# A split weight's low part: one VectorE subtraction, or a ScalarE negative and an adding DMA

## The chip, the cores and the metric

The kernel runs on one core of a Trainium2 chip. Its time is the device time of one execution in microseconds (us); the number given for a kernel is the median of several executions. A profile is one execution recorded by the hardware profiler.

The engines in the profile are PE (TensorE; PEld is its loading of weights into the array), DVE (VectorE), ACT (ScalarE), POOL (GpSimd) and SP (which here only starts transfers). Each works through its own list of instructions in order and waits on semaphores for the others.

## The reference

Two layers of a decoder trunk on 256 positions of width 1024, all in float32. In each layer:

```python
h = h + hybrid_mixer(rmsnorm(h), ...)   # retention and an SSD scan side by side, merged by gates
h = h + swiglu(rmsnorm(h), ...)         # gate and up of width 2816, then down
```

and a last rmsnorm. The mixer multiplies the normed input by one wide matrix `w_in` and cuts the product into `q, k` (1024 columns each), `v, g_ret, z` (2048 each), `xbc` (3072), `dt` (32) and two gates (1024 each). What matters here is `xbc`: it goes through a causal convolution of four taps along the positions and a silu, and is cut into `xs` (2048 columns), `bm` and `cm` (512 each) for the scan:

```python
xbc = jax.nn.silu(causal_dwconv(xbc, conv_w, conv_b))
xs, bm, cm = jnp.split(xbc, [SSD_INNER, SSD_INNER + SSD_BC], axis=-1)
```

## The kernel before

**Float32 by halves.** TensorE multiplies in a format (fp32r) that keeps fewer bits than float32. So every operand is split into a high part, rounded to fp32r, and a low part, the rest. A product is the sum of three: high by high, high by low, low by high. A piece of weights is 128 x 1024 numbers (512 KB). It is loaded from memory into a tile `raw` by a DMA on SP's queue (line 488), then split in `split_piece`: ScalarE copies it into `wh`, which rounds it (line 506), and VectorE writes `wl = raw - wh` (line 527).

**Jobs.** The weights are cut into jobs. The ones of the convolution and of q and k are called `fm` jobs: 256 columns of `w_in`, in two pieces of four blocks of 128 rows each. `fm_job` runs two halves of 128 columns. In each half it goes through the eight row blocks k = 0 to 7, and for each k does a matmul of `wh` with high and low input side by side (512 columns, line 988; line 991 for the last one, which closes the half) and one of `wl` with the high input (256 columns, line 989). The first piece serves k = 0 to 3 and the second k = 4 to 7, in both halves. A half has eight matmuls of line 989; the fifth is the first that needs the `wl` of the second piece.

A layer's mixer list has 20 fm jobs: four `bc`, four `q`, four `k` and eight `xs` (named by group and half: `("xs", 0, 0)` to `("xs", 3, 1)`). From the first `q` on the order is q, k, xs in turn four times, then the `g` jobs with the other four `xs` jobs between them, then `ret`. The list ends with `z`, `ssd` and `wo`, and the FFN's jobs follow.

**Sevens.** Some products are done by a seven-product scheme, whose weight sums are built by `wino_sums`. Some of these sums are made by VectorE; others by a DMA that POOL issues and that adds a piece from memory to a tile already filled (line 416, `accum_op=ALU.add`). These are the only adding transfers before the change, 48 of them, all into float32 tiles.

**Buffers.** There are four `raw` buffers and seven pairs of `wh` and `wl` (`HB = 7`, semaphore `hlS`). Pieces take the pairs in the order of the jobs (`turn.before.taken`), so a piece can be split as soon as the piece seven places ahead of it has been used by TensorE. A `raw` buffer is given back when the split is done.

**Order.** The order of each engine's instructions is planned when the kernel is built, by a small event simulation (`Flow`). Each stream of work yields an `Op` with an engine, a cost in ns and a priority; the free engine takes the ready `Op` of the lowest number. Transfers are costed by `fl.transfer`, on a single queue. The order that comes out is fixed; on the chip only the waits decide when things run. A changed cost or a moved operation may therefore change the order of everything behind it.

**A form that exists but is not used.** `split_piece` takes a `src`. With it, ScalarE writes the negative of `wh` into `wl`, POOL issues a DMA that adds the weights from memory, and the low part is there when the DMA has landed. Jobs whose index is in a tuple `apart` get `src`; before the change each of these tuples is empty.

Of the kernel before, what the change touches and what calls it, by code (L numbers as in the profile page):

```python
# [16 lines left out]
P = 128  # L17
# [175 lines left out]
def trunk_kernel(  # L193
# [4 lines left out]
):  # L198
    nc = tc.nc
    HB, RB, TAIL, WARM = 7, 4, 5, 2  # L200
    APART, LATE = (), 2500.0
    SLOW, MT_SLACK = 1500.0, 800.0
    ADDS = 600.0
    ZS_PR, SAVE, DEC_AT = 1.0, 2000.0, 9000.0
    PR0, SLACK = 1.6, 2500.0
    BESIDE = (8, 10, 12, 14, 11, 11, 9, 24, 44, 46)
    APARTS, SUMS_PR = {}, 3.5
    cp = ctx.enter_context(tc.tile_pool(name="cp", bufs=1))
    wp = ctx.enter_context(tc.tile_pool(name="wp", bufs=HB))
    big = ctx.enter_context(tc.tile_pool(name="big", bufs=4))  # L210
# [80 lines left out]
    ALONE = ("11", "t1", "t2", "22", "t3", "21", "t4")  # L291


    AMID = ("*", "*", "*", "*", "11", "*", "t1", "*", "t2", "22", "*", "t3", "*", "21", "*", "t4")

    SMID = ("*", "*", "11", "*", "t1", "*", "t2", "22", "*", "t3", "21", "t4")


    RMID = ('*', '*', '*', '*', '*', '*', '11', '*', 't1', 't2', '22', 't3', '21', 't4')
    RET_FIRST, RET_APART, RET_PR = (decS, new_dec), (), 0.0  # L300

    class Turn:
        def __init__(self):
# [2 lines left out]
    def group(*adds):  # L306

        of = len(jobs)
        got_turns, got_specs, stars = [], [], []
        for add in adds:  # L310
            t, f, at = add(of)
            if stars:

                t, f = ([(stars[i] if i < len(stars) else 1.0 + i, v) for i, (_, v) in enumerate(e)] for e in (t, f))
            stars = stars or at
            got_turns += t
            got_specs += f
        for into, got in ((turns, got_turns), (specs, got_specs)):
            for _, v in sorted(got, key=lambda e: e[0]):
                if into is turns and turns:  # L320
                    v.before = turns[-1]
                into.append(v)
# [152 lines left out]
    def out_srcs(w):  # L475
        return [(w[k0 : k0 + P, :], 1, D) for k0 in range(0, w.shape[0], P)]
# [14 lines left out]
            raw = yield Op("sp", 450, load, job)  # L491
            fl.spawn(land(raw, fl.transfer(512 * k * n, 4 * k * n)))

    def split_piece(raw, m, turn, pr, src=None):

        if turn.before:
            yield turn.before.taken  # L500
        yield hlS
        fl.set(turn.taken)

        def split_h():
            wh = wp.tile([P, D], F32R, tag="wh", name="wh")
            nc.scalar.activation(out=wh[:, :m], in_=raw[:, :m], func=AF.Copy)  # L506
            return wh

        wh = yield Op("act", 0.833 * m + 92, split_h, pr)

        def negative():
            wl = wp.tile([P, D], F32R, tag="wl", name="wl")
            nc.scalar.activation(out=wl[:, :m], in_=wh[:, :m].bitcast(F32), func=AF.Copy, scale=-1.0)
            return wl

        def add(wl):
            nc.gpsimd.dma_start(out=wl[:, :m], in_=src, accum_op=ALU.add)

        if src is not None:
            wl = yield Op("act", 0.833 * m + 92, negative, pr)  # L520
            yield Op("pool", 1050, lambda: add(wl), pr)
            yield fl.transfer(512 * m, 4 * m, 2.2) - ADDS
            return wh[:, :m], wl[:, :m]

        def split_l():
            wl = wp.tile([P, D], F32R, tag="wl", name="wl")
            nc.vector.tensor_tensor(out=wl[:, :m], in0=raw[:, :m], in1=wh[:, :m].bitcast(F32), op=ALU.subtract)  # L527
            return wl

        wl = yield Op("dve", 1.04 * m + 69, split_l, pr)  # L530
        return wh[:, :m], wl[:, :m]

    def splitter(turn, k, n, ev, job, src, sem):
        def land(raw, landed):
            yield landed
            wh, wl = yield from split_piece(raw, k * n, turn, job - 0.7, src)
            fl.release(sem)
            fl.set(ev, tuple(a.rearrange("p (k n) -> p k n", k=k) for a in (wh, wl)))
        return land

# [516 lines left out]
    def out_wino(op, nk, at, tag, order, post, add, ops):  # L1057
# [74 lines left out]
        for t in range(NT):  # L1132
            for n in range(2):
# [5 lines left out]

    FFN = [[("plain", 0)],
           [("fm", 1)],
           [("seven", (2,), ("t3", "t4"))],
           [("fm", 3)],
           [("seven", (4,), ("t3", "t4"))],
           [("fm", NPAIR)]]
    DIRECT = ()
    DOWN_APART = ()


    MIXER = [("v", 0), ("gr", 0), ("bc", 0, 0), ("v", 1), ("bc", 0, 1), ("v", 2), ("bc", 1, 0), ("v", 3),
# [5 lines left out]

    TM = {"v": 0, "g": 4, "z": 8, "gs": 12}
    FM = {"q": 0, "k": 4, "xs": 8, "bc": 16}  # L1160


    MIXERS = [MIXER[:2] + [MIXER[i ^ 1] for i in range(2, 10)] + MIXER[10:], MIXER]

    def add_layer_jobs(l):
        def srcs_of(kind, *at):
            if kind == "gr":
                return tm_srcs(w_gr[l, at[0]])
            if kind in FM:
                return fm_srcs(w_fm[l, FM[kind] + at[0] + (at[0] + at[1] if len(at) > 1 else 0)])  # L1170
            if kind in ("ret", "ssd", "wo"):
                return out_srcs({"ret": ret_out, "ssd": ssd_out, "wo": w_o}[kind][l])
            return tm_srcs(w_tm[l, TM[kind] + at[0]], kper=1 if l == 0 and (kind, *at) == ("v", 0) else 2)

        def adds_of(kind, *at, order=MIXED):
            if kind == "seven":
                c = TM[at[0]] + at[1]
                return [sevens(w_tm[l, c], w_tm[l, c + 1], added=at[2], order=order, slots=None)]
            return [plain((srcs_of(kind, *at), APARTS.get((kind, *at), ())))]

        for m in MIXERS[l]:
            if m == ("ret",):
                group(sevens(w_rw[l, 0], w_rw[l, 1], added=("t3", "t4"), order=RMID, first=RET_FIRST),
                      plain((out_srcs(ret_out[l])[8:], RET_APART)))
            elif m == ("ssd",):
                group(sevens(w_sw[l, 0], w_sw[l, 1], added=("t3", "t4"), order=SMID, slots=(ccS, new_cc)),
                      plain((out_srcs(ssd_out[l])[8:], ())))
            elif isinstance(m, tuple):
                for add in adds_of(*m, order=ALONE):
                    group(add)  # L1190
            else:
                group(*(chain(*(a for j in stream for a in adds_of(*j))) for stream in m))
        for members in FFN:
            adds = []
            for kind, *at in members:
                if kind == "seven":
                    adds.append(chain(*(sevens(w_gate_up[l, 0, c], w_gate_up[l, 1, c], added=at[1], order=ALONE if len(members) == 1 else ASIDE,
                                               slots=(ccS, new_cc)) for c in at[0])))
                elif kind == "fm":
                    adds.append(plain(*((srcs, APART) for c in at for srcs in gf_srcs(l, c))))  # L1200
                else:
                    adds.append(plain(*((srcs, APART) for c in at for srcs in gate_up_srcs(l, c))))
            group(*adds)
        lone = [s for k, s in enumerate(out_srcs(w_down[l])) if k // 4 not in (DW, DW + 1)]
        group(sevens(w_dw[l, 0], w_dw[l, 1], added=("t3", "t4"), order=AMID, slots=(ccS, new_cc)),
              plain((lone, DOWN_APART)))

    def params(l, done):
        prm = sp.tile([P, 3, NH], F32, tag="prm", name="prm", bufs=1)
# [21 lines left out]
    def layer(l, mix, nxt, opening=None):  # L1231
# [537 lines left out]
            to = yield gated[t]  # L1769
            yield tt(512, j, to[:, nsl], u, sgr[t][:, nsl], ALU.mult)  # L1770

        run["ret"] = lambda: out_wino(yr, 16, 0, "O", RMID, ret_post, add_r, rops)


        yz = Operand(SG, ["Y", "Y", "C", "C"])
# [108 lines left out]
        def ssd_job():  # L1884
            for i in range(2):
                xT.drop(i)
            for t in range(NT):
                fl.spawn(restore(t))
            fl.spawn(ffn.start(at_job[0]))
            fl.spawn(ffn.sums(at_job[0] + 2))  # L1890
            return out_wino(yz, 16, 0, "A", SMID, ssd_post, add_m, zops)

        run["ssd"] = ssd_job

# [113 lines left out]
                return [m for c in at for m in fm_pair(c)]  # L2008
            return [((lambda m=m: tm_job(ffn.xT, m)), 1) for c in at for m in pair(c)]

        last = max(i for i, g in enumerate(FFN) for kind, *_ in g if kind == "seven")
        for i, members in enumerate(FFN):
            if i == 0:
                yield from tm_pair(ffn.xT, *((m, 512, 2) for m in pair(members[0][1])))
            else:
                yield from together(*[ffn_jobs(*m) for m in members])
            if i == last:
                ffn.drop_sums()
# [6 lines left out]

        ops = {q: Event() for q in ALONE}
        fl.spawn(seven_sums(ops, gu, (DW, DW + 1), "D", at_job[0] - 1.2))
        yield from out_wino(gu, FF // P, DW, "D", AMID, add_to(nxt), add_h, ops)

    def rotary_half(rotary, dst, which, done):  # L2030
        part = Event()
# [189 lines left out]
```

## Time and profile before

| | |
|---|---|
| times of three executions | 1252.75, 1253.32, 1255.91 us; median 1253.32 |
| span of the profiled execution | 1251.4 us, from its first to its last instruction (its time as the others are measured is not given beside it) |
| instructions | 17609 |
| granted TensorE clock | 0.999 in the mean |
| DMA | 266.27 MB, in the mean 213 GB/s |

The page gives busy times by engine, groups of instructions by line, and the chain of work that ended last. Other views used below: the timeline (instructions in order, with the idle time before each and what ended it in brackets), the waits (who waited for whom, with total, number and longest), and windows (busy time by engine in given stretches). PE's matmuls overlap in these records: each stands with some 0.39 us, while the next begins 0.23 us after it.

### The profile page before, as it was taken

What the parts mean: (1) busy time and instruction counts of PE and PEld (TensorE: products, weight loads), DVE (VectorE), ACT (ScalarE), POOL (GpSimd) and SP (SyncE); (2) the same over time, 40 slices, a digit from 0 to 9 for tenths busy, and PEclk for the clock granted to TensorE, in tenths of its full rate; (3) what the DMA queues carried; (4) which work ended last, traced back from release to release, by engine and by line L of the source; (5) the groups of instructions that cost most, each with busy time, mean ns of one, the idle gap of its engine ahead of it and who ended that gap; (6) DMA issues with size and microseconds to landing.
All of it is one profiled execution on the core that took longest, in us unless ns stands there. A gap on an engine that the chain in (4) does not pass through costs nothing.

```text
span 1251.4 us, 17609 instructions
## 1 busy us (share of the span) xinstructions
PE 1241.9 (99%) x6286; PEld 1052.4 (84%) x6286; DVE 1108.2 (89%) x1516; ACT 882.7 (71%) x1305; POOL 71.1 (6%) x92
## 2 busy tenths in 40 slices
PE   9999999999999999999999999999999999999997
PEld 8889888888888888888888898888888888888886
DVE  6998989789999979999788888888899998899995
ACT  6866876977776666776586676878877674776753
POOL 0000000001012001001000000000010110010000
PEclk9999999999999999999999999999999999999999
DMA  8758555456768658877776475555577786688872
GB/s 293 248 146 284 184 180 174 153 194 192 253 238 226 229 178 231 297 212 219 249 257 227 124 256 167 188 172 163 208 186 234 243 234 213 225 209 249 289 204 86
DMA packets 76343, 266.27 MB, mean 213 GB/s; under 512 B 8768, under 2 KB 9024, under 8 KB 76256
## 3 DMA queue, kind: packets, MB, share of 16 engines
q1 hardware_dynamic: 68416, 237.25, 55.7%
q0 software_dynamic: 7552, 27.38, 11.8%
q8 instruction: 49, 0.80, 0.2%
q10 hardware_dynamic: 288, 0.52, 0.1%
q14 instruction: 38, 0.31, 0.1%
HBM read 262.96 MB, written 2.16 MB: 212 GB/s over the span
## 4 chain that ended last, share of the span: by engine, by line
PE 92%; ACT 3%; issue 2%; DMA 1%; DVE 0%; POOL 0%; SPq 0%; POOLq 0%; ACTq 0%
PE acc L543 19%; PE acc L544 19%; PE acc L545 19%; PE acc L988 15%; PE acc L989 9%; PE tr L640 2%; PE yps L1700 2%; PE acc L991 2%; ACT wh L506 1%; ACT seg L1668 1%; PE acc L1422 1%; PE tr L1593 1%; PE ips L1687 1%; DMA raw<-in_w_tm_dram 1%; DMA raw<-in_w_gr_dram 0%
## 5 line engine op out<-in xcount | busy, mean ns | idle before, releaser
L506 ACT ACTIVATE wh<-raw 128x1024 fp32r<-128x1024 f32 (+2 forms) x388 | 397.0, 1035 | 150.6 <-PE acc L545 36.3
L527 DVE TENSOR_TENSOR wl<-raw,wh 128x1024 fp32r<-128x1024 f32 (+2 forms) x388 | 458.9, 1196 | 48.5 <-ACT wh L506 46.6
L988 PE MATMUL acc<-xT,wh 128*128 128x512 f32 x840 | 304.2, 400 | 0.0
L989 PE MATMUL acc<-xT,wl 128*128 128x256 f32 x960 | 251.6, 281 | 0.0
L543 PE MATMUL acc<-wh,xT 128*128 128x512 f32 (+1 forms) x568 | 220.6, 388 | 0.0
L545 PE MATMUL acc<-wh,xT 128*128 128x512 f32 (+1 forms) x568 | 216.1, 380 | 0.0
L544 PE MATMUL acc<-wl,xT 128*128 128x512 f32 (+1 forms) x568 | 216.1, 380 | 0.0
L989 PEld LDWEIGHTS acc<-xT,wl 128*128 128x128 f32 x960 | 181.2, 189 | 10.1
L988 PEld LDWEIGHTS acc<-xT,wh 128*128 128x128 f32 x840 | 158.0, 188 | 32.2
L544 PEld LDWEIGHTS acc<-wl,xT 128*128 128x128 f32 x568 | 106.7, 188 | 20.4 <-issue 1.2
L543 PEld LDWEIGHTS acc<-wh,xT 128*128 128x128 f32 x568 | 106.7, 188 | 19.8 <-issue 1.6
L545 PEld LDWEIGHTS acc<-wh,xT 128*128 128x128 f32 x568 | 106.6, 188 | 19.5
L506 ACT ACTIVATE wh<-raws 128x1024 fp32r<-128x1024 f32 x80 | 83.5, 1056 | 31.7 <-DVE raws L230 12.5
L527 DVE TENSOR_TENSOR wl<-raws,wh 128x1024 fp32r<-128x1024 f32 x80 | 96.4, 1222 | 8.9 <-ACT wh L506 8.7
L543 PE MATMUL acc<-wh,A 128*128 128x512 f32 x224 | 89.8, 401 | 0.2
L545 PE MATMUL acc<-wh,A 128*128 128x512 f32 x224 | 87.4, 390 | 0.0
L544 PE MATMUL acc<-wl,A 128*128 128x512 f32 x224 | 87.3, 390 | 0.0
L233 DVE SCALAR_TENSOR_TENSOR cc<-cc,cv 128x255 f32<-128x255 f32 (+1 forms) x144 | 67.3, 479 | 3.0 <-ACT cc L223 2.1
L543 PE MATMUL acc<-wh,C 128*128 128x512 f32 (+1 forms) x152 | 59.2, 389 | 0.0
L544 PE MATMUL acc<-wl,C 128*128 128x512 f32 (+1 forms) x152 | 58.3, 384 | 0.2 <-DVE wl L527 0.2
L545 PE MATMUL acc<-wh,C 128*128 128x512 f32 (+1 forms) x152 | 58.2, 383 | 0.0
L223 ACT ACT_TABLE_LOAD x41 | 52.6, 1283 | 6.1 <-DVE cc L233 5.4
(197 smaller groups left out, 2006.8 us busy)
## 6 DMA issues: line engine op xcount, KB each, us to landing
raw<-in_w_tm_dram SPq DMA_DIRECT2D x104, 512.0 KB, 4.2
raw<-in_w_fm_dram SPq DMA_DIRECT2D x80, 512.0 KB, 4.3
raw<-in_w_gf_dram SPq DMA_DIRECT2D x40, 512.0 KB, 4.5
raw<-in_w_gate_up_dram SPq DMA_DIRECT2D x32, 512.0 KB, 5.8
raw<-in_w_down_dram SPq DMA_DIRECT2D x28, 512.0 KB, 4.5
raw<-in_w_gr_dram SPq DMA_DIRECT2D x24, 352.0 KB, 3.7
seg<-acs SPq DMA_DIRECT2D x16, 512.0 KB, 4.9
raw<-in_ret_out_dram SPq DMA_DIRECT2D x16, 512.0 KB, 4.3
```

Of the source, the lines that this page charges most:

```text
L223: return Op("act", cost, lambda: nc.scalar.activation(out=out, in_=in_, func=func, **kw), pr, TABLES.get(func))
L233: return Op("dve", 1.04 * n + 130, lambda: nc.vector.scalar_tensor_tensor(out=out, in0=in0, scalar=scalar, in1=in1, op0=op0, op1=op1), pr)
L506: nc.scalar.activation(out=wh[:, :m], in_=raw[:, :m], func=AF.Copy)
L527: nc.vector.tensor_tensor(out=wl[:, :m], in0=raw[:, :m], in1=wh[:, :m].bitcast(F32), op=ALU.subtract)
L543: nc.tensor.matmul(ps, lhsT=lh, rhs=rh, start=first, stop=False, **kw)
L544: nc.tensor.matmul(ps, lhsT=lh, rhs=rl, start=False, stop=False, **kw)
L545: nc.tensor.matmul(ps, lhsT=ll, rhs=rh, start=False, stop=last, **kw)
L640: nc.tensor.transpose(out=ps[:, j * P : (j + 1) * P], in_=src[:, j * P : (j + 1) * P], identity=ident)
L988: nc.tensor.matmul(a, lhsT=wh[:, k % 4, fsl], rhs=x[:, k % 4, :, :], start=k == 0, stop=False)
L989: nc.tensor.matmul(a[:, :SEQ], lhsT=wl[:, k % 4, fsl], rhs=xh[:, k % 4, :], start=False, stop=False)
L991: nc.tensor.matmul(a, lhsT=wh[:, k % 4, fsl], rhs=x[:, k % 4, :, :], start=False, stop=True)
L1700: nc.tensor.matmul(ps[:, i * HD : (i + 1) * HD], lhsT=sg[:, i, :], rhs=xdt[:, i * HD : (i + 1) * HD], start=True, stop=True)
```

## The change

The low part of the second piece of all 16 `xs` jobs (eight in each layer) is made with `src`. The rest of the diff turns constants into tables by layer that hold the same values (the mixer lists, the FFN lists, the orders of the sevens). Cut to what acts:

```diff
-    APARTS, SUMS_PR = {}, 3.5
+    APARTS, SUMS_PR = {(0, 'xs', 0, 0): (1,), (0, 'xs', 0, 1): (1,), ..., (1, 'xs', 3, 1): (1,)}, 3.5
...
-    def split_piece(raw, m, turn, pr, src=None):
+    def split_piece(raw, m, turn, pr, src=None, sem=None):
...
         if src is not None:
             wl = yield Op("act", 0.833 * m + 92, negative, pr)
+            if sem:
+                fl.release(sem)
             yield Op("pool", 1050, lambda: add(wl), pr)
             yield fl.transfer(512 * m, 4 * m, 2.2) - ADDS
             return wh[:, :m], wl[:, :m]
...
-            wh, wl = yield from split_piece(raw, k * n, turn, job - 0.7, src)
-            fl.release(sem)
+            wh, wl = yield from split_piece(raw, k * n, turn, job - 0.7, src, sem)
+            if src is None:
+                fl.release(sem)
...
-            return [plain((srcs_of(kind, *at), APARTS.get((kind, *at), ())))]
+            return [plain((srcs_of(kind, *at), APARTS.get((l, kind, *at), ())))]
```

With `src`, a `raw` buffer is now given back after the negative, not after the transfer.

For each of these pieces one instruction of VectorE goes (line 527), and there come one of ScalarE, one DMA issue on POOL's queue, and one transfer of 512 KB that reads the weights a second time and adds them to `wl` in place.

More of the change, by code (lines that the diff above doesn't have):

```diff
@@ L200, in trunk_kernel @@
     HB, RB, TAIL, WARM = 7, 4, 5, 2
-    APART, LATE = (), 2500.0
+    LATE = 2500.0
     SLOW, MT_SLACK = 1500.0, 800.0
@@ L206, in trunk_kernel @@
     BESIDE = (8, 10, 12, 14, 11, 11, 9, 24, 44, 46)
-    APARTS, SUMS_PR = {}, 3.5
+    APARTS, SUMS_PR = {(0, 'xs', 0, 0): (1,), (0, 'xs', 0, 1): (1,), (0, 'xs', 1, 0): (1,), (0, 'xs', 1, 1): (1,), (0, 'xs', 2, 0): (1,), (0, 'xs', 2, 1): (1,), (0, 'xs', 3, 0): (1,), (0, 'xs', 3, 1): (1,), (1, 'xs', 0, 0): (1,), (1, 'xs', 0, 1): (1,), (1, 'xs', 1, 0): (1,), (1, 'xs', 1, 1): (1,), (1, 'xs', 2, 0): (1,), (1, 'xs', 2, 1): (1,), (1, 'xs', 3, 0): (1,), (1, 'xs', 3, 1): (1,)}, 3.5
     cp = ctx.enter_context(tc.tile_pool(name="cp", bufs=1))
@@ L291, in trunk_kernel @@
     ALONE = ("11", "t1", "t2", "22", "t3", "21", "t4")
[L294 to L300, printed above, removed]
+    AMIDS = [('*', '*', '*', '*', '11', '*', 't1', '*', 't2', '22', '*', 't3', '*', '21', '*', 't4'), ('*', '*', '*', '*', '11', '*', 't1', '*', 't2', '22', '*', 't3', '*', '21', '*', 't4')]
+    SMIDS = [('*', '*', '11', '*', 't1', '*', 't2', '22', '*', 't3', '21', 't4'), ('*', '*', '11', '*', 't1', '*', 't2', '22', '*', 't3', '21', 't4')]
+    RMIDS = [('*', '*', '*', '*', '*', '*', '11', '*', 't1', 't2', '22', 't3', '21', 't4'), ('*', '*', '*', '*', '*', '*', '11', '*', 't1', 't2', '22', 't3', '21', 't4')]
+    ADDED = {(0, 'ret'): ('t3', 't4'), (0, 'ssd'): ('t3', 't4'), (0, 'down'): ('t3', 't4'), (1, 'ret'): ('t3', 't4'), (1, 'ssd'): ('t3', 't4'), (1, 'down'): ('t3', 't4')}
+    RET_FIRST, RET_PR = (decS, new_dec), 0.0
     class Turn:
@@ L1138, in out_wino @@
                 fl.spawn(done(t, n))
[L1142 to L1147, printed above, removed]
-    DIRECT = ()
-    DOWN_APART = ()
-    MIXER = [("v", 0), ("gr", 0), ("bc", 0, 0), ("v", 1), ("bc", 0, 1), ("v", 2), ("bc", 1, 0), ("v", 3),
[5 rows of a table removed]
+    FFNS = [[[('plain', 0)], [('fm', 1)], [('seven', (2,), ('t3', 't4'))], [('fm', 3)], [('seven', (4,), ('t3', 't4'))], [('fm', 5)]], [[('plain', 0)], [('fm', 1)], [('seven', (2,), ('t3', 't4'))], [('fm', 3)], [('seven', (4,), ('t3', 't4'))], [('fm', 5)]]]
+    DIRECT = ()
+    MIXER0 = [('v', 0), ('gr', 0), ('v', 1), ('bc', 0, 0), ('v', 2), ('bc', 0, 1), ('v', 3), ('bc', 1, 0), [[('seven', 'gs', 0, ('t3',))], [('gr', 1), ('gr', 2)]], ('bc', 1, 1), ('q', 0), ('k', 0), ('xs', 0, 0), ('q', 1), ('k', 1), ('xs', 0, 1), ('q', 2), ('k', 2), ('xs', 1, 0), ('q', 3), ('k', 3), ('xs', 1, 1), ('g', 0), ('xs', 2, 0), ('g', 1), ('xs', 2, 1), ('g', 2), ('xs', 3, 0), ('xs', 3, 1), ('g', 3), ('ret',), ('z', 0), ('z', 1), ('z', 2), ('z', 3), ('ssd',), ('wo',)]
+    MIXER1 = [('v', 0), ('gr', 0), ('bc', 0, 0), ('v', 1), ('bc', 0, 1), ('v', 2), ('bc', 1, 0), ('v', 3), ('bc', 1, 1), [[('seven', 'gs', 0, ('t3',))], [('gr', 1), ('gr', 2)]], ('q', 0), ('k', 0), ('xs', 0, 0), ('q', 1), ('k', 1), ('xs', 0, 1), ('q', 2), ('k', 2), ('xs', 1, 0), ('q', 3), ('k', 3), ('xs', 1, 1), ('g', 0), ('xs', 2, 0), ('g', 1), ('xs', 2, 1), ('g', 2), ('xs', 3, 0), ('xs', 3, 1), ('g', 3), ('ret',), ('z', 0), ('z', 1), ('z', 2), ('z', 3), ('ssd',), ('wo',)]
+    MIXERS = [MIXER0, MIXER1]
     TM = {"v": 0, "g": 4, "z": 8, "gs": 12}
     FM = {"q": 0, "k": 4, "xs": 8, "bc": 16}
-    MIXERS = [MIXER[:2] + [MIXER[i ^ 1] for i in range(2, 10)] + MIXER[10:], MIXER]
     def add_layer_jobs(l):
@@ L1178, in adds_of @@
                 return [sevens(w_tm[l, c], w_tm[l, c + 1], added=at[2], order=order, slots=None)]
-            return [plain((srcs_of(kind, *at), APARTS.get((kind, *at), ())))]
+            return [plain((srcs_of(kind, *at), APARTS.get((l, kind, *at), ())))]
         for m in MIXERS[l]:
             if m == ("ret",):
-                group(sevens(w_rw[l, 0], w_rw[l, 1], added=("t3", "t4"), order=RMID, first=RET_FIRST),
-                      plain((out_srcs(ret_out[l])[8:], RET_APART)))
+                group(sevens(w_rw[l, 0], w_rw[l, 1], added=ADDED[l, "ret"], order=RMIDS[l], first=RET_FIRST),
+                      plain((out_srcs(ret_out[l])[8:], APARTS.get((l, "ret"), ()))))
             elif m == ("ssd",):
-                group(sevens(w_sw[l, 0], w_sw[l, 1], added=("t3", "t4"), order=SMID, slots=(ccS, new_cc)),
-                      plain((out_srcs(ssd_out[l])[8:], ())))
+                group(sevens(w_sw[l, 0], w_sw[l, 1], added=ADDED[l, "ssd"], order=SMIDS[l], slots=(ccS, new_cc)),
+                      plain((out_srcs(ssd_out[l])[8:], APARTS.get((l, "ssd"), ()))))
             elif isinstance(m, tuple):
@@ L1192, in add_layer_jobs @@
                 group(*(chain(*(a for j in stream for a in adds_of(*j))) for stream in m))
-        for members in FFN:
+        for members in FFNS[l]:
             adds = []
@@ L1199, in add_layer_jobs @@
                 elif kind == "fm":
-                    adds.append(plain(*((srcs, APART) for c in at for srcs in gf_srcs(l, c))))
+                    adds.append(plain(*((srcs, APARTS.get((l, kind, c), ())) for c in at for srcs in gf_srcs(l, c))))
                 else:
-                    adds.append(plain(*((srcs, APART) for c in at for srcs in gate_up_srcs(l, c))))
+                    adds.append(plain(*((srcs, APARTS.get((l, kind, c), ())) for c in at for srcs in gate_up_srcs(l, c))))
             group(*adds)
         lone = [s for k, s in enumerate(out_srcs(w_down[l])) if k // 4 not in (DW, DW + 1)]
-        group(sevens(w_dw[l, 0], w_dw[l, 1], added=("t3", "t4"), order=AMID, slots=(ccS, new_cc)),
-              plain((lone, DOWN_APART)))
+        group(sevens(w_dw[l, 0], w_dw[l, 1], added=ADDED[l, "down"], order=AMIDS[l], slots=(ccS, new_cc)),
+              plain((lone, APARTS.get((l, "down"), ()))))
     def params(l, done):
@@ L1770, in add_r @@
             yield tt(512, j, to[:, nsl], u, sgr[t][:, nsl], ALU.mult)
-        run["ret"] = lambda: out_wino(yr, 16, 0, "O", RMID, ret_post, add_r, rops)
+        run["ret"] = lambda: out_wino(yr, 16, 0, "O", RMIDS[l], ret_post, add_r, rops)
         yz = Operand(SG, ["Y", "Y", "C", "C"])
@@ L1890, in ssd_job @@
             fl.spawn(ffn.sums(at_job[0] + 2))
-            return out_wino(yz, 16, 0, "A", SMID, ssd_post, add_m, zops)
+            return out_wino(yz, 16, 0, "A", SMIDS[l], ssd_post, add_m, zops)
         run["ssd"] = ssd_job
@@ L2009, in ffn_jobs @@
             return [((lambda m=m: tm_job(ffn.xT, m)), 1) for c in at for m in pair(c)]
-        last = max(i for i, g in enumerate(FFN) for kind, *_ in g if kind == "seven")
-        for i, members in enumerate(FFN):
+        last = max(i for i, g in enumerate(FFNS[l]) for kind, *_ in g if kind == "seven")
+        for i, members in enumerate(FFNS[l]):
             if i == 0:
@@ L2027, in layer @@
         fl.spawn(seven_sums(ops, gu, (DW, DW + 1), "D", at_job[0] - 1.2))
-        yield from out_wino(gu, FF // P, DW, "D", AMID, add_to(nxt), add_h, ops)
+        yield from out_wino(gu, FF // P, DW, "D", AMIDS[l], add_to(nxt), add_h, ops)
     def rotary_half(rotary, dst, which, done):
```

5 rows, old and new, of the table MIXER are left out of this document.

## The prediction, made before the changed kernel was run

> **What bounds the kernel now.** I read the page's first two parts, then TensorE's own waits, then the stretches in which the 16 changed jobs are made and used.
>
> ```profile
> span 1251.4 us, 17609 instructions
> PE 1241.9 (99%) x6286; PEld 1052.4 (84%) x6286; DVE 1108.2 (89%) x1516; ACT 882.7 (71%) x1305; POOL 71.1 (6%) x92
> ```
>
> TensorE is busy for 1241.9 of 1251.4 us. The 9.5 us that are left lie almost all at the two ends, as the first and the last TensorE row of the timeline show: nothing runs before 1.32 us, and the last matmul ends at 1244.03 + 0.39 = 1244.42, 7.0 us before the end. That is 8.3 us, so about 1.2 us is open in between.
>
> ```profile
> 1.32 5.91 PE L2094 MATMUL idle<-zeros 128*128 128x384 f32 x19 [1.32 <-DVE mhalf L2071]
> ...
> 1244.03 0.39 PE L545 MATMUL acc<-wh,Y 128*128 128x512 f32 x1
> ```
>
> Busy time hides short waits, because a matmul's end is modelled and overlaps the next. So I also read what TensorE's weight loads wait for. Over the whole run the one wait for a VectorE split (line 527) is 0.8 us in two cases:
>
> ```profile
> PEld acc L544 <- DVE wl L527: 0.8, 2, 0.5
> ```
>
> The changed jobs lie between 112 and 290 us (layer 0) and 729 and 908 us (layer 1). The waits inside these two stretches, and the busy time in six windows that cover them (columns: window, length, then busy time and count of each engine, the last three granted clock, DMA share and GB/s):
>
> ```profile
> PEld acc L543 <- ACT sil L223: 1.0, 2, 0.5
> PEld acc L543 <- issue: 0.5, 2, 0.2
> PEld acc L544 <- issue: 0.5, 2, 0.2
> PEld acc L1422 <- issue: 0.4, 1, 0.4
> ...
> 112.00:175.00 63.00, 62.91 (x360) 55.08 (x359) 53.85 (x88) 46.51 (x75) 1.84 (x2) 1.00 0.64 212
> 175.00:240.00 65.00, 65.00 (x353) 55.69 (x352) 53.15 (x84) 52.23 (x99) 3.56 (x2) 1.00 0.55 170
> 240.00:290.00 50.00, 49.88 (x267) 41.98 (x266) 45.98 (x69) 41.85 (x68) 0.00 (x0) 1.00 0.57 190
> ...
> sum 357.00, PE 356.67 PEld 307.06 DVE 303.66 ACT 280.46 POOL 8.36; mean PE 59.45 PEld 51.18 DVE 50.61 ACT 46.74 POOL 1.39
> ```
>
> TensorE is idle for 0.33 of 357 us there. In layer 0 its weight loads wait 2.4 us in all, and none of it for VectorE; the largest share is for ScalarE (1.0 us). VectorE, the engine that is relieved, is 85% busy in these windows, but TensorE does not wait for it.
>
> **The change, part by part.** Each of the 16 xs jobs has two pieces of weights. For the second one, the difference raw minus wh is no longer a VectorE instruction; ScalarE writes -wh into wl, and a DMA issued by POOL reads the weights from memory again and adds them to wl.
>
> ```profile
> L506 ACT ACTIVATE wh<-raw 128x1024 fp32r<-128x1024 f32 (+2 forms) x388 | 397.0, 1035 | 150.6 <-PE acc L545 36.3 <-DMA raw<-in_w_tm_dram 25.6 <-issue 13.8
> L527 DVE TENSOR_TENSOR wl<-raw,wh 128x1024 fp32r<-128x1024 f32 (+2 forms) x388 | 458.9, 1196 | 48.5 <-ACT wh L506 46.6
> ```
>
> *VectorE, removed.* 16 instructions of 1.2 us: 19 us less, of 303.66 in the windows (85% to 80%). Worth nothing on the path, as TensorE has no wait for VectorE there.
>
> *ScalarE, added.* 16 negatives. None exists before; the nearest row is the split of the same 128x1024 shape (line 506, 1.04 us in the mean, 1.06 in the single rows below). That is 17 us more: 280.46 to 297 of 357, 79% to 83%. The cover is ScalarE's idle time, and the tightest place is the end of the stretch, where TensorE does wait for ScalarE (the 1.0 us above, for sil). The last two negatives of a layer come by the split at 250.04. The idle times from there up to the wait stand in square brackets; the row of a window, the last, shows how full ScalarE (23.88 of 25 us) is behind them, and the row before it, of the chain, is the sil that TensorE waits for:
>
> ```profile
> 250.04 1.06 ACT L506 ACTIVATE wh<-raw 128x1024 fp32r<-128x1024 f32 x1 [1.30 <-PE acc L545]
> 251.44 0.60 ACT L223 ACTIVATE cc<-cc,cv 128x256 f32<-128x256 f32 x1 [0.34 <-DVE cc L230]
> 252.76 1.06 ACT L506 ACTIVATE wh<-raw 128x1024 fp32r<-128x1024 f32 x1 [0.72 <-PE acc L545]
> 255.48 1.06 ACT L506 ACTIVATE wh<-raw 128x1024 fp32r<-128x1024 f32 x1 [1.66 <-PE acc L545]
> ...
> 261.95 0.60 ACT L223 ACTIVATE C<-tr 128x512 f32<-128x512 f32 x1 [1.32 <-PE tr L1593]
> ...
> 264.59 0.60 ACT L223 ACTIVATE A<-tr 128x512 fp32r<-128x512 f32 x1 [1.56 <-PE tr L640]
> 266.24 1.06 ACT L506 ACTIVATE wh<-raw 128x1024 fp32r<-128x1024 f32 x1 [1.04 <-PE acc L988]
> ...
> 286.17 0.50 ACT sil L223
> ...
> 265.00:290.00 25.00, 24.88 (x121) 20.33 (x120) 21.43 (x33) 23.88 (x44) 0.00 (x0) 1.00 0.60 209
> ```
>
> After 251.1 that is 0.34 + 0.72 + 1.66 + 1.32 + 1.56 + 1.04 = 6.6 us, against 2.1 us for both negatives. So ScalarE is back in step by 267 us, ahead of the full stretch that ends in the wait. Cost: nothing; if that cover were gone, 2.1 us in each layer (a rival below).
>
> *POOL, added.* 16 DMA issues. The issues of the same kind before the change (line 416), one whole group, the landing times of all of line 416, and one that directly follows a split:
>
> ```profile
> L416 POOL DMA_DIRECT2D cc<-in_w_gate_up_dram x8: 854/865/913, 483.5 to 1147.8; - x8
> ...
> DMA to landing us min/median/max: 5.1/5.6/9.2
> ...
> 296.38 0.86 POOL L416 DMA_DIRECT2D raw<-in_w_rw_dram  x1 [0.24 <-ACT wh L506]
> POOL rr L243 <- DVE ms L238: 140.7, 4, 77.3
> ```
>
> 14 us of POOL's time, where it works for 8.36 us in 357. What stands behind such an issue on POOL's queue is the four rr instructions of a layer, and they wait 140.7 us for VectorE anyway; a microsecond more reaches nobody.
>
> *Latency of the low part: the step on which the forecast rests.* It was wh, then 1.2 us on VectorE. It becomes wh, 1.06 us on ScalarE, 0.24 us to POOL, and 5.6 us from issue to landing: 6.9 us after wh instead of 1.2 or more. TensorE first needs it in the fifth matmul of line 989 of the job (a job's half ends with a matmul of line 991). I matched pieces by counting the rows of lines 506 and 989 in the order of the job list. The tightest of the 16 is the first xs job of each layer, then the fourth:
>
> ```profile
> 123.14 1.06 ACT L506 ACTIVATE wh<-raw 128x1024 fp32r<-128x1024 f32 x1 [0.70 <-DMA raw<-in_w_fm_dram]
> ...
> 132.25 0.40 PE L991 MATMUL acc<-xT,wh 128*128 128x512 f32 x1
> 134.12 0.28 PE L989 MATMUL acc<-xT,wl 128*128 128x256 f32 x1
> ...
> 742.08 2.25 ACT L506 ACTIVATE wh<-raw 128x1024 fp32r<-128x1024 f32 x2
> 753.60 0.28 PE L989 MATMUL acc<-xT,wl 128*128 128x256 f32 x1
> ...
> 226.47 1.07 ACT L506 ACTIVATE wh<-raw 128x1024 fp32r<-128x1024 f32 x1
> 240.04 0.28 PE L989 MATMUL acc<-xT,wl 128*128 128x256 f32 x1
> ```
>
> Layer 0, first job: wh ends at 124.20, the issue can begin at 125.50, and the weight load of the matmul at 134.12 comes some 0.2 us before it, at 133.9. The landing may take 8.4 us. Layer 1: wh ends at 743.14 (the row holds two; this piece is the first), issue at 744.44, needed at 753.4: 9.0 us. Layer 0, fourth job: wh ends at 227.54, issue at 228.84, needed at 239.8: 11.0 us. The 13 others have at least as much as that. With the median landing the slack is 2.8, 3.4 and 5.4 us. At the longest landing of the trace, 9.2, TensorE would wait 0.8 and 0.2 us: 1.0 in the whole run. Bounds of this step: 0 and 1.0 us; a gain is excluded, since it only makes wl later. I take 0, as 5.6 is the median of the same issues.
>
> *DMA engines, added.* 16 transfers of 512 KB.
>
> ```profile
> q1 hardware_dynamic: 68416, 237.25, 55.7%
> q0 software_dynamic: 7552, 27.38, 11.8%
> 125.00:131.00 6.00, 6.00 (x36) 5.21 (x35) 5.96 (x12) 3.95 (x7) 0.00 (x0) 1.00 0.84 272
> ```
>
> POOL's queue took 11.8% of 1251.4 for 27.38 MB: 5.4 us for a MB, so 2.8 us of all 16 engines for each of the 16 (plain loads on SP's queue take 1.5). That is 45 us in 357: the shares of 0.55 to 0.64 rise to 0.68 to 0.77. Room is left, least of all at the first job, where the share from 125 to 131 us is 0.84 already; there the add and the raw loads behind it slow each other. This is why I keep the longest landing as a bound. The raw loads of the following jobs have a lead like those above and lose at most 2.8 us of it.
>
> *SP's queue.* A raw buffer comes free after wh instead of after VectorE's instruction, so 16 loads may start 1.2 us or more sooner. Worth nothing, since TensorE does not wait for them.
>
> *Order.* The builder plans each engine's order by a cost model, and every choice after the first changed piece can fall otherwise. The tables hold the same jobs in the same order. I take 0, and 1 us to either side, by the 1.2 us that is open inside the run and the 1.0 us of possible lateness.
>
> A rule of the Trainium skill speaks against the change. The page SBUF — State Buffer, section "SBUF: two separate sides", warns that POOL cannot write the descriptors of its DMAs while VectorE runs an instruction that uses both of its ports. By that rule an issue could be held for one VectorE instruction, 1.2 us, and a landing would take 6.8 us, still inside the 8.4. The trace does not show it: with VectorE 89% busy the issues of the group above took 854 to 913 ns, all alike.
>
> *Sum.* 0 on TensorE's path, 1251.4 us of span again. The times shown for the runs are 1252.75, 1253.32 and 1255.91; the median is 1.9 us above that span, which is the part around it. Forecast 1253.3 us.
>
> **The rivals.**
>
> *The add lands too late (slower).* Place: the first xs job of each layer. The new transfers write into an fp32r tile, while all of line 416 write into f32 tiles (raw, raws, cc, dec), so their landing is not known. At twice the median, 11.2 us, TensorE waits 2.8 + 2.2 + 0.2 = 5.2 us: 1258.5. It passes 0.3% (3.8 us) once a landing takes 10.6 us, since (10.6 - 8.4) + (10.6 - 9.0) = 3.8. Against it: 5.1 to 9.2 in 48 cases. For it: the share of 0.84 at that place. On the type, the page DMA: Bandwidth & Descriptors of the Trainium skill, section on SWDGE, HWDGE and iDMA, states that a transfer into float32r always casts; it gives no price, and no run here has one.
>
> *ScalarE becomes the bound (slower).* If the plan puts two negatives into ScalarE's work between 267 and 287 us, the wait for sil grows by 2.1 us in each layer: 1257.5. For it: the 1.0 us wait there. Against it: the 6.6 us of idle time just ahead.
>
> *VectorE's relief shortens TensorE's waits (faster).* If every wait of the weight loads in these stretches went, 2.4 us in layer 0 and, by an estimate, the same in layer 1, the time would be 1248.5. Against it: none of them is for VectorE.
>
> *More room in TensorE than its busy time says (faster).* In the windows weight loads fill 307.06 of 357 us; if the other 50 could be used, 1203. Against it are the waits, which sum to 2.4 us in 178. The page Perfetto Trace Analysis of the Trainium skill, section "Identifying the Most-Contended Engine", takes that measure, not matmul time, for TensorE's headroom.
>
> **How the numbers follow.** A measurement here can tell about 0.3%, 3.8 us, from no change. Forecast, within 0.3%: 82 in 100. Late add 6, ScalarE 4, a worse order elsewhere 2: slower by over 0.3%, 12 in 100. Relief together with a luckier order 5, hidden room 1: faster, 6 in 100. The range runs from 1250.0 (most of the waits gone, within the spread of the runs) to 1258.5 (the late add) and takes in the 1.0 us of the longest landing and the ScalarE rival.
>
> **What would show it.** Line 527 loses 16 instructions, ScalarE has 16 more of about 1.06 us, line 416's kind of issue comes 16 times with a landing of 5 to 9 us, and TensorE's busy time stays near 1242 with the same small waits. Wrong if the weight loads of line 989 wait for that DMA near 134 or 753 us, if their wait for sil near 286 or 904 us grows, or if TensorE's waits turn up far from the changed jobs.

## The result and the profile after

The changed kernel takes 1258.62 us in the median of four runs (1257.50 to 1259.96), the kernel before 1253.46 beside it (four runs, 1252.75 to 1255.91): a ratio of 1.0038, 95% interval 1.0026 to 1.0050 (over all executions; the quotient of the two medians is 1.0041). It is slower by 0.4%, and 1258.62 lies just past the upper end of the range. Two executions in this document were far slower than all others of their kernel and are left out: one of the kernel before (1541.96 us), and one of the kernel with the dearer price below (5262.70 us), which is its profiled one, so its trace is not used.

The profiled execution has a span of 1255.7 us against 1251.4. From its page, the engines, the split on VectorE, POOL's queue and the new transfers (last number: median us from issue to landing):

```profile
span 1255.7 us, 17642 instructions
PE 1242.9 (99%) x6286; PEld 1051.4 (84%) x6286; DVE 1091.4 (87%) x1500; ACT 894.1 (71%) x1319; POOL 89.0 (7%) x108
q0 software_dynamic: 9856, 35.77, 15.6%
L527 DVE TENSOR_TENSOR wl<-raw,wh 128x1024 fp32r<-128x1024 f32 (+2 forms) x372 | 438.8, 1192 | 54.4 <-ACT wh L504 53.4
wl<-in_w_fm_dram POOLq DMA_DIRECT2D x16, 512.0 KB, 7.9
```

The edits are there: 16 splits fewer on line 527 (388 to 372) and 16 issues more on POOL (92 to 108); VectorE works 17 us less. TensorE's busy time is 1.0 us more than it was, 1242.9 against 1241.9, while the last matmul starts at 1248.63 instead of 1244.03:

```profile
1248.63 0.39 PE L546 MATMUL acc<-wh,Y 128*128 128x512 f32 x1
```

So 4.6 us went between matmuls somewhere. Windows find the place (window, length, then busy time and count of PE, PEld, DVE, ACT and POOL, then clock, DMA share, GB/s). First two windows of before, behind the changed jobs of each layer:

```profile
290.00:450.00 160.00, 160.00 (x769) 133.12 (x768) 151.39 (x191) 105.58 (x149) 14.74 (x20) 1.00 0.71 218
908.00:1066.00 158.00, 158.00 (x759) 131.41 (x758) 149.43 (x187) 103.67 (x145) 14.63 (x20) 1.00 0.71 219
```

The same two of the changed kernel, and the two that hold the changed jobs:

```profile
112.00:290.00 178.00, 177.78 (x977) 153.28 (x976) 144.34 (x234) 150.50 (x250) 10.13 (x12) 1.00 0.71 215
290.00:450.00 160.00, 159.02 (x761) 131.02 (x760) 148.90 (x185) 101.07 (x144) 17.79 (x20) 1.00 0.69 214
730.00:908.00 178.00, 177.77 (x975) 153.62 (x974) 141.67 (x225) 146.10 (x243) 10.07 (x12) 1.00 0.71 216
908.00:1066.00 158.00, 155.86 (x743) 128.30 (x743) 146.79 (x183) 99.97 (x141) 17.11 (x19) 1.00 0.71 218
```

Where the changed jobs are made and used, TensorE is as full as it was (177.78 and 177.77 of 178, against 177.79 and 177.88). The loss is in the two stretches behind them, the retention product, `z` and the scan: busy time falls from 160.00 to 159.02 and from 158.00 to 155.86, with 8 and 16 matmuls fewer in the window. With the weight matmuls of both traces paired by their place in the list, the changed kernel is 0.55 us ahead at 272 us, 1.4 behind from 450 to 785, still 1.4 at 905, and 4.6 from 1063 to the end: 2.0 us are lost in the first stretch and 3.2 in the second.

TensorE's weight loads tell what it waited for there (us in total, times, longest):

```profile
PEld tr L641 <- issue: 3.0, 5, 0.8
PEld ips L1677 <- PE acc L546: 1.9, 2, 1.0
PEld acc L544 <- ACT sx L223: 1.9, 2, 1.5
...
PEld acc L545 <- DVE wl L527: 1.8, 5, 0.6
```

None of these loads is of line 990, which uses the new low parts, and none waits for their DMA. Two of these rows have none like them before: the wait for the copy `sx` by ScalarE, and the one of `ips`, a product of the scan. The timeline has the longest of each: 946.96 (ScalarE) and 356.37, where the bracket names VectorE's `xdt`; the list above puts the same wait down to TensorE's own earlier matmul.

```profile
356.37 1.10 PE L1677 MATMUL ips<-xdt,cbm 128*128 128x512 f32 x2 [0.54 <-DVE xdt L230]
...
946.96 0.51 PE L544 MATMUL acc<-wh,Y 128*128 128x512 f32 x1 [1.04 <-ACT sx L223]
```

With the usual 0.23 us from one matmul to the next taken off, the four largest such stops of layer 1 are 1.2 us (946.96), 0.8 (977.30), and 0.6 and 0.2 at the transposes `tr` at 1044 and 1047. All are far from the changed jobs, and those are the same instructions as before. What differs is their order: set side by side, TensorE's list differs from the one before in some 70 places (stretches of neighbouring instructions), VectorE's in some 180, ScalarE's in some 100 and SP's in fewer than 10.

### The profile page after: what moved, and what is told of

Its sections match the earlier page's. It is cut to its first block, busy times and chain, and to the rows that moved or that the text cites. A ratio compares the mean times of both kernels' runs of the same rounds, so it can differ in the third digit from the quotient of the medians.

```text
span 1255.7 us, 17642 instructions
## 1 busy us (share of the span) xinstructions
PE 1242.9 (99%) x6286; PEld 1051.4 (84%) x6286; DVE 1091.4 (87%) x1500; ACT 894.1 (71%) x1319; POOL 89.0 (7%) x108
## 4 chain that ended last, share of the span: by engine, by line
PE 82%; DVE 7%; ACT 3%; issue 3%; DMA 3%; POOL 0%; SPq 0%; POOLq 0%; DVEq 0%; ACTq 0%
PE acc L544 17%; PE acc L546 17%; PE acc L545 17%; PE acc L989 15%; PE acc L990 8%; DVE wl L527 3%; PE acc L992 2%; PE tr L641 2%; PE yps L1690 2%; ACT wh L504 1%; DVE D L230 1%; DMA raw<-in_w_tm_dram 1%; DMA raw<-in_w_rw_dram 1%; ACT seg L1658 1%; DMA raws<-in_w_sw_dram 1%
## 5 line engine op out<-in xcount | busy, mean ns | idle before, releaser
L527 DVE TENSOR_TENSOR wl<-raw,wh 128x1024 fp32r<-128x1024 f32 (+2 forms) x372 | 438.8, 1192 | 54.4 <-ACT wh L504 53.4
```

## The experiments

Two theories stood at the start. P: the loss is in the order that the planner comes to once costs and queues differ. M: it is in what the new instructions do (ScalarE's time, the late landing, the DMA load). All ratios are to the kernel before, run on the same chip, with 95% intervals.

**Old order, new instructions; new order, old instructions.** The first keeps the plan of before and, where VectorE's subtraction stood in it, emits the negative and the adding DMA. TensorE's and SP's lists are those of before. The second keeps the plan of after and emits the subtraction in the negative's place, with no adding DMA.

```diff
 # old order, new instructions (before)
         def split_l():
+            if late is not None:
+                wl = negative()
+                nc.gpsimd.dma_start(out=wl[:, :m], in_=late, accum_op=ALU.add)
+                return wl
 # new order, old instructions (after)
         def negative():
-            nc.scalar.activation(out=wl[:, :m], in_=wh[:, :m].bitcast(F32), func=AF.Copy, scale=-1.0)
+            nc.vector.tensor_tensor(out=wl[:, :m], in0=raw[:, :m], in1=wh[:, :m].bitcast(F32), op=ALU.subtract)
         def add(wl):
-            nc.gpsimd.dma_start(out=wl[:, :m], in_=src, accum_op=ALU.add)
+            pass
```

> The order planned for the kernel before, instruction for instruction on TensorE and SP, but each of the 16 low parts is made by ScalarE's negative and the adding transfer. Theory P (the loss is in the order that the planner lays down behind the changed jobs): no loss, within 0.1% of before, about 1253.5 us; no wait of TensorE for ips, sx or D around 326 to 427 and 947 to 1048 us. Theory M (the new instructions themselves, by ScalarE's time, by DMA traffic or by late landings, delay the work behind): the whole loss, about 1258 us.

> The order planned for the changed kernel on TensorE and SP, but the 16 low parts are made by VectorE's subtraction, at the place in the plan where ScalarE's negative stood; no negatives and no adding transfers into wl. Theory P: the whole loss stays, about 1258 us, with the same waits near 947, 977 and 1044 us. Theory M: back to 1253.5 us.

Measured: 1254.39 us, 1.0007 (0.9998 to 1.0016), and 1260.82 us, 1.0060 (1.0047 to 1.0072). The two windows, of the old order with the new instructions:

```profile
290.00:450.00 160.00, 160.00 (x771) 133.17 (x770) 151.37 (x192) 105.57 (x148) 14.34 (x20) 1.00 0.70 218
908.00:1066.00 158.00, 158.00 (x762) 131.53 (x760) 149.20 (x188) 103.89 (x144) 14.62 (x20) 1.00 0.71 220
```

and of the new order with the old instructions:

```profile
290.00:450.00 160.00, 158.74 (x758) 130.34 (x757) 148.74 (x187) 100.81 (x142) 17.86 (x20) 1.00 0.70 217
908.00:1066.00 158.00, 155.20 (x741) 127.66 (x740) 148.40 (x185) 101.09 (x141) 17.13 (x19) 1.00 0.72 218
```

P holds and M falls. The new instructions in the old order cost nothing that can be told from no change; the new order without them has the whole loss. The first run beside the change is the cleanest pair: the work is the same, the order alone differs, and 1.0007 stands against 1.0038. Nothing is gained either: 16 subtractions off VectorE are worth 0 in the old order. Whether they give back part of the loss in the new one (1.0038 against 1.0060) is not settled: the intervals touch, and the subtractions stand at places that no plan gave them.

**Only the planner's price.** The kernel before, with every instruction as it was, but the 16 subtractions priced 300 ns dearer, or cheaper, in the plan.

```diff
-        wl = yield Op("dve", 1.04 * m + 69, split_l, pr)
+        wl = yield Op("dve", 1.04 * m + 69 + more, split_l, pr)   # more = 300.0 or -300.0 for these 16
```

> The kernel before with the same instructions; only the planner's price of VectorE's subtraction of these 16 pieces is 300 ns higher, which moves the order on every engine (71 places on TensorE against 72 for the change). Theory P: another order is another time, most likely a loss of 0.1 to 0.5%, 1254.5 to 1260 us, since the order before was left with next to no waits. Theory M: 1253.5 us, as no instruction differs.

> As the kernel with the higher price, but 300 ns lower (82 places on TensorE). Theory P: a time of its own, 1254.5 to 1260 us. Theory M: 1253.5 us.

Measured: dearer 1268.26 us (three executions), 1.0110 (1.0095 to 1.0126); cheaper 1260.51 us, 1.0054 (1.0041 to 1.0067). P has the side right and the size too low: both lie above its 1254.5 to 1260 us. The waits of the second are on other instructions than in the changed kernel, VectorE's this time:

```profile
PEld acc L546 <- DVE A L230: 3.7, 2, 1.8
```

A number that moves no instruction to another engine costs 0.54 or 1.10%, where the change costs 0.38. So the loss does not need this change: leaving the order of before is enough for it.

**A price nearer the chip's.** The landing that was measured (7.9 us) is later than the plan's. Here the changed kernel's plan has these landings 1750 ns later.

```diff
-            yield fl.transfer(512 * m, 4 * m, 2.2) - ADDS
+            yield fl.transfer(512 * m, 4 * m, 2.2) - ADDS + 1750.0
```

> The changed kernel; only the planner's price for the landing of the 16 adds is raised by 1750 ns, to what was measured (median 7.9 us from issue). No instruction differs, the order does (30 places on TensorE). If the loss came from the wrong price of the landings, the right one takes it away: 1254 us. Theory P (any order that was not searched for loses): 1255 to 1262 us, no better than the change on the whole.

Measured: 1267.86 us, 1.0108 (1.0094 to 1.0123). A truer price of this one item made a worse order, and again P's range (1255 to 1262 us) was too low. TensorE's longest wait, two cases:

```profile
PEld acc L544 <- ACT sx L223: 8.0, 2, 4.0
```

and ScalarE's timeline ahead of the one in layer 1:

```profile
943.59 2.45 ACT L1658 ACTIVATE seg<-seg,ax 128x128 f32<-128x128 f32 x8 [4.66 <-DMA seg<-acs]
...
950.21 0.58 ACT L223 ACTIVATE sx<-acc 128x512 f32<-128x512 f32 x1
```

**Half the jobs, or one layer.** The change in the last four xs jobs of each layer only, and in layer 1 only (the tuple `APARTS` cut to these).

> The change in the last four xs jobs of each layer alone (half of the instructions). A loss in proportion to the instructions would be 2.5 us, 1256 us. Theory P: a time that follows no proportion, anywhere from 1253.5 to 1262 us, lost in 290 to 450 and 908 to 1066 us.

> The change in layer 1 alone; layer 0 has the order of before. Theory P: no loss until 735 us; behind it a loss of its own in 908 to 1066 us, 0.5 to 5 us, as the order there is neither that of before nor that of the change. Theory M was dropped after the first four kernels.

Measured: the last four 1267.40 us, 1.0102 (1.0088 to 1.0117), more than twice the loss with half the instructions, and above P's 1262; layer 1 only 1258.16 us, 1.0032 (1.0020 to 1.0044), within P's 0.5 to 5 us. The two windows of the latter:

```profile
290.00:450.00 160.00, 160.00 (x770) 133.20 (x770) 151.33 (x192) 105.89 (x148) 14.73 (x20) 1.00 0.69 217
908.00:1066.00 158.00, 155.77 (x743) 128.30 (x742) 147.31 (x184) 100.23 (x141) 17.13 (x19) 1.00 0.70 219
```

The layer that keeps its order keeps its time, 160.00 of 160; the other loses as before. The waits of the last-four kernel:

```profile
PEld acc L545 <- ACT sx L224: 9.0, 2, 5.5
...
PEld acc L991 <- DMA wl<-in_w_fm_dram: 2.1, 1, 2.1
```

The second row is the late add that the prediction feared, once, in an order that is not the changed kernel's (with the dearer landing there is one of 0.5 us).

**More relief for VectorE.** By now a theory D said that VectorE, which is 95% busy in 290 to 450 us (151.39 of 160), is what a worse order has no room for, so that relieving it there should win the loss back; its rival O, that TensorE stands behind late transfers and ScalarE however free VectorE is. In the changed kernel's order, 12 more low parts of each layer (four of `ret`, eight of `z`) are made by the negative and an adding DMA in the place of the subtraction.

> The changed kernel with its own order on TensorE and SP; in addition the low parts of 12 weight pieces of each layer that are split between 290 and 390 us (four of ret, eight of z) are made by ScalarE's negative and an adding transfer at the place where VectorE's subtraction stood. Theory D (the new order loses because VectorE, full in that stretch, gets gaps there that it cannot make up before TensorE needs it): the waits near 326, 356, 947 and 977 us go, those near 423 and 1044 us stay, 1255 to 1256 us. Theory O (the order itself puts TensorE's instructions ahead of data that comes late by transfers or ScalarE, however free VectorE is): the waits stay, 1258 us or more, since ScalarE and the DMA engines get more work.

Measured: 1289.25 us, 1.0273 (1.0258 to 1.0287): D is far off, and O, which said 1258 us or more, gave no size. VectorE falls to 132.61 of 160 us, and TensorE now waits for the adds themselves. Its waits, a window, and the landing of all 40:

```profile
PEld acc L550 <- DMA wl<-in_w_tm_dram: 6.3, 4, 3.2
PEld acc L550 <- DMA wl<-in_ret_out_dram: 4.5, 2, 2.2
```

```profile
290.00:450.00 160.00, 151.58 (x701) 123.70 (x700) 132.61 (x170) 105.47 (x146) 25.10 (x29) 0.97 0.80 230
```

```profile
DMA to landing us min/median/max: 5.2/7.6/12.2
```

It does not tell D from O, since it brought in a cost of its own: 10.8 us of waits for the adds, of some 34 lost; the rest is not taken apart, and the granted clock, 0.97 in this window, is lower too. It shows that the cover of 8 us and more is a property of the xs jobs: these pieces are used sooner, and the same latency stops TensorE.

**One instruction's place.** In the changed kernel, in the dearer landing and in the last four, the longest stop is at the same point: TensorE waits for one copy `sx<-acc`, which frees an accumulator. ScalarE runs its list in order, so what stands ahead of that copy counts. The kernel before, ScalarE's timeline:

```profile
931.48 2.43 ACT L1668 ACTIVATE seg<-seg,ax 128x128 f32<-128x128 f32 x8
...
935.36 1.28 ACT L223 ACT_TABLE_LOAD   x1
936.65 1.06 ACT L223 ACTIVATE seg<-seg 128x1024 f32<-128x1024 f32 x1
...
942.77 0.57 ACT L223 ACTIVATE sx<-acc 128x512 f32<-128x512 f32 x1
```

The changed kernel:

```profile
932.62 2.45 ACT L1658 ACTIVATE seg<-seg,ax 128x128 f32<-128x128 f32 x8 [0.50 <-DMA seg<-acs]
936.10 0.60 ACT L223 ACTIVATE sx<-acc 128x512 f32<-128x512 f32 x1 [1.03 <-DVE tail L230]
938.38 1.06 ACT L504 ACTIVATE wh<-raw 128x1024 fp32r<-128x1024 f32 x1 [1.68 <-DMA raw<-in_w_rw_dram]
940.14 1.06 ACT L504 ACTIVATE wh<-raw 128x1024 fp32r<-128x1024 f32 x1 [0.70 <-DMA raw<-in_w_rw_dram]
...
944.07 1.28 ACT L223 ACT_TABLE_LOAD   x1
945.36 1.06 ACT L223 ACTIVATE seg<-seg 128x1024 f32<-128x1024 f32 x1
946.33 0.58 ACT L223 ACTIVATE sx<-acc 128x512 f32<-128x512 f32 x1
```

Before, table load and exp come early and the waits for transfers are short; after, ScalarE first stands idle 3.9 us (0.50 + 1.03 + 1.68 + 0.70) and then does table load and exp, 2.3 us, just ahead of the copy that TensorE needs. Theory S: their place makes the stop. Rival T: the stop is what late transfers leave, and the place only shows it. Test: emit table load and exp (in the two slower orders also the eight relus, which wait for the transfer) right behind that copy. TensorE's, VectorE's, POOL's and SP's lists stay as they are; on ScalarE the copy alone, in the other two orders it and the two splits ahead of it, come forward.

```diff
             if (g, t) == (3, 0):
+                for op in (relus, exp):          # changed kernel: (exp,)
+                    op.fn = lambda fn=op.fn: behind.append(fn)
...
+            copy.fn = lambda fn=copy.fn: (fn(), flush())[0]    # sx<-acc, then what waits in behind
```

> The changed kernel with one move on ScalarE and nothing else: for the scan's last group, first half (the one job near 324 and 945 us), the table load and the exp of seg are issued behind the copy sx<-acc instead of ahead of it. All other instructions and their order on every engine are those of the changed kernel. Theory S (TensorE's stall at 946.96 us, 1.2 us, is there because the new order puts table load and exp, 2.3 us, ahead of the one copy that frees the accumulator): that stall and the wait of acc for ACT sx (1.9 us in two cases) are gone, TensorE's other stalls stay, and the time falls by 1 to 1.5 us to about 1257.3. Rival T (TensorE's stalls are what a later transfer or VectorE allows, and ScalarE's place in line only shows it): the stall stays, or comes back within 15 us at a matmul that waits for seg, and the time stays at 1258.6.

> The same move on the kernel with the dearer landing in the plan (1267.9 us), where TensorE stalls 3.7 us at this point in each layer: the eight relus and the exp of seg, which wait 4.7 us for the transfer seg<-acs, are issued behind the two splits and the copy sx<-acc that stood behind them. Theory S: both stalls of 3.7 us are gone or under 0.5 us, ScalarE's wait for seg<-acs shrinks from 4.7 to under 1 us, and the time falls by 6 to 7.5 us to about 1261. Rival T: the relus come later, so the scan's product for this group and all that waits for it is late, the stalls come back there, and the time stays above 1266.

> The same move on the kernel in which only the last four xs jobs of a layer are changed (1267.4 us), where the stalls at this point are 3.2 and 5.3 us and ScalarE waits 6.2 us for the transfer. Theory S: both stalls go, and the time falls by 7.5 to 8.5 us to about 1259.5. Rival T: above 1265.

Measured: the changed kernel 1259.02 us, 1.0042 (1.0029 to 1.0054), against 1.0038 without the move; the dearer landing 1265.63, 1.0093 (1.0078 to 1.0109), against 1.0108; the last four 1266.25, 1.0098 (1.0084 to 1.0112), against 1.0102. None of S's gains of 1 to 8.5 us came: the medians moved by +0.4, -2.2 and -1.2 us, and each interval overlaps that of the kernel without the move (1265.63 is also 0.4 us under T's 1266). In the changed kernel the stop at the copy is gone, and 12.5 us later there is one of 0.8 us that was not there. It waits for VectorE, not for `seg` as T had it:

```profile
959.48 0.50 PE L551 MATMUL acc<-wl,xT 128*128 128x512 f32 x1 [0.65 <-DVE wl L533]
```

In the order of the dearer landing, ScalarE after the move, and TensorE:

```profile
939.45 1.06 ACT L510 ACTIVATE wh<-raw 128x1024 fp32r<-128x1024 f32 x1 [2.03 <-DMA raw<-in_w_rw_dram]
944.12 1.06 ACT L510 ACTIVATE wh<-raw 128x1024 fp32r<-128x1024 f32 x1 [3.61 <-DMA raw<-in_w_rw_dram]
945.09 0.58 ACT L223 ACTIVATE sx<-acc 128x512 f32<-128x512 f32 x1
...
954.07 0.57 ACT L223 ACTIVATE sx<-acc 128x512 f32<-128x512 f32 x1
...
954.70 0.50 PE L550 MATMUL acc<-wh,Y 128*128 128x512 f32 x1 [3.24 <-ACT sx L223]
```

The copy is done 5 us sooner (945.09 against 950.21), that stop of 3.7 us is gone, and 3.4 us came back at the next copy, at 954.07. S falls as a cause: in this order ScalarE still stands dry for 5.6 us (2.03 + 3.61), then has all its work at once, and whatever is last in it is late.

Why the transfers are late can be followed one step further, to the load of `seg` (the scan's decay factors) for which the relus wait. SP issues it, in order, once TensorE's `yps` of the group before has freed a buffer; SP's rows before, after, and with the dearer landing:

```profile
925.39 0.33 SPq L1658 DMA_DIRECT2D seg<-acs  x1
```

```profile
927.49 0.33 SPq L1648 DMA_DIRECT2D seg<-acs  x1
```

```profile
933.63 0.42 SPq L1648 DMA_DIRECT2D seg<-acs  x1
```

The load goes out 2.1 and 8.2 us later than before, but TensorE itself, its weight matmuls paired as above, is by then 1.3 and 8.2 us behind. Counted from TensorE's place the load is 0.8 us later in the changed kernel and not later at all with the dearer landing, which loses more. So it is not a late issue that makes the longer stop. What differs is how long the load takes: 4.0, 5.1 and 9.9 us from issue to landing for these three rows, and 11.5 in the last four. Layer 0 has the same: 4.0, 5.2, 10.0 and 9.4 us. All 16 loads of `seg` with the dearer landing:

```profile
DMA to landing us min/median/max: 3.7/5.4/10.0
```

In the two slower orders SP has issued a raw load 0.4 us ahead of this one; before and after, none for 9 us and more. That this place among the transfers is the cause agrees with these rows, but it is argued and not shown, and a slow load alone is not enough: with the cheaper price it took 8.6 and 9.6 us, and TensorE's longest waits there are for VectorE. No run moved a transfer alone.

No version beat the kernel before; the old order with the new instructions equals it.

## Why the prediction was wrong

**The step that failed is *Order*:** "every choice after the first changed piece can fall otherwise ... I take 0, and 1 us to either side". The runs put the whole loss there: 0 with the old order, 0.60% with the new order alone, and 0.32 to 1.10% for the five further plans (two prices of the subtraction, one of the landing, half the jobs, one layer). For this change the term is 5 us and not 0 to 1, and no other plan tried came out faster than the old one. The two numbers I bounded it by (1.2 us open inside the run, 1.0 us of possible lateness) are the slack of the present order; they say nothing of another one. A schedule with 1.2 us open in 1240 has next to nothing to gain from another order and much to lose; all six other orders lost. Which chain of events makes each of them lose stays open: the stops are at other places in other orders, and moving one instruction did not bring the time back.

**The rival "a worse order elsewhere" had 2 in 100** and no place or price. The profile could have given it a place; a price, only runs of other orders give. The windows that I quoted cover the changed jobs; the next one shows VectorE at 151.39 of 160 us, 95% busy where my windows gave it 85% in the mean, with TensorE at 160.00, and it is there that the loss fell (that VectorE's fullness is the reason was not shown). The last sentence of the prediction, that it is wrong "if TensorE's waits turn up far from the changed jobs", is what happened.

**Latency of the low part: size wrong, result right.** I took a landing of 5.6 us with 9.2 as the longest. The new transfers' own row:

```profile
L515 POOL DMA_DIRECT2D wl<-in_w_fm_dram x16: 857/886/921, 123.9 to 871.8; - x16
...
DMA to landing us min/median/max: 5.3/7.9/11.2
```

The median is 2.3 us later and the longest beyond the upper bound of 9.2. No load of line 990 waits for it, but in part by luck. At the first job of each layer the landing took 8.5 us, where the prediction had 8.4 and 9.0 to spare. With the rows counted in the order of the job list, the tile was there 1.5 and 0.5 us ahead of its matmul, in layer 0 with the help of an add that went out 1.6 us sooner than expected (123.94 instead of 125.50). The longest, 11.2 us, fell on the last job of layer 0, which had 5.5 us left. (By the same count the row at 240.04, which the prediction gives to the fourth xs job, is the sixth's.) The late-add rival (1258.5) gave nearly the measured time, by a mechanism that was not there: that agreement is luck.

**What held.** VectorE's 17 us and ScalarE's 16 negatives cost and give nothing where they are: the stretches of the changed jobs are full before and after. POOL's issues took 857 to 921 ns and delayed nobody. So what the page SBUF — State Buffer of the Trainium skill, section "SBUF: two separate sides", says of descriptor writing is not seen here either, with VectorE 87% busy; which of VectorE's instructions use both ports, no view here shows. ScalarE's negatives (1.05 us, estimated at 1.06) did not become the bound: TensorE's waits for `sil`, which the rival would lengthen, are no longer among its waits.

## What to carry to other kernels

Where the instruction order is planned from costs and the bound engine is already 99% busy, test an edit with the old order kept and the new instructions put in its places: here that run, beside the change itself, said that the edit was worth nothing and the loss was the order's. A changed price with no changed instruction is the control that gives the scale of such a loss (here 0.5 to 1.1%), and a forecast for a re-planned kernel should start from that scale, not from 0. Clearing the longest wait did not help here: in the two orders shown, another came up within 13 us.

The page Perfetto Trace Analysis of the Trainium skill, section "Optimization Strategies", advises to optimize the engine that the matmul engine waits for. The runs here limit that: with ScalarE's copy moved up TensorE no longer waited for it at 946.96 us, and the time stayed the same (1.0042 against 1.0038).

## What the runs showed of the hardware

An adding transfer of 512 KB into an fp32r tile took 7.9 us in the median from issue to landing (5.3 to 11.2); in the same profile those into the other tiles took 5.6 (5.2 to 9.4):

```profile
DMA to landing us min/median/max: 5.2/5.6/9.4
```

With the old order the new ones took 7.5 us (5.4 to 10.0). Whether the type or the place among other transfers makes the difference was not tried. The page DMA: Bandwidth & Descriptors of the Trainium skill, section "Anatomy of one DMA — SWDGE (gpsimd) path", gives a fit of 2.0 us plus bytes over 436e3; for 524288 bytes that is an estimate of 3.2 us, below every one of these landings.
